# Rotary embedding by pairs of rows: twelve pairs moved to TensorE, three PSUM banks, and transfers of two tiles

## The chip, the cores and the metric

The kernel runs on one core of one Trainium2 chip. The metric is the device time of one execution in microseconds; the figure for the kernel before is the median of three runs, 164.04 us. The profile is of one execution and counts from its first to its last instruction (its span).

The engines are named as in the profile: PE is TensorE (PEld its loading of weights), DVE is VectorE, ACT is ScalarE, POOL is GpSimd, SP is SyncE, which issues the large transfers. The transfers of all queues run on the core's 16 DMA engines. SBUF is the on-chip memory, of 128 partitions; PSUM is the small memory that TensorE writes, of eight banks, each of 512 fp32 values a partition.

## The reference

The input `x` is 16 x 512 x 1024 fp32 (33.6 MB); every row of 1024 is 16 heads of 64. `cos` and `sin` are 512 x 32, one row for each position.

```python
x = x.reshape(batch, seq, num_heads, head_dim)
x1, x2 = x[..., :half_dim], x[..., half_dim:]
cos = cos[None, :, None, :]
sin = sin[None, :, None, :]
rotated = np.concatenate([x1 * cos - x2 * sin, x1 * sin + x2 * cos], axis=-1)
```

With the two halves of each head swapped, this is one product and one sum for each element: `out = x * cos + swapped(x) * (-sin, +sin)`. Every byte is read once and written once.

## The kernel before

**Tiles.** A tile is two batches (`BP = 2`): 64 partitions for each, and 8 rows (`R = 8`) of 1024 in each partition, so 8192 fp32 or 32 KB a partition and 4.19 MB a tile. There are eight tiles (`NT`) and five SBUF buffers for them (`NB`, `bufs` at L80). The result is written over `x` in the buffer and stored from there. Tiles 5, 6 and 7 are loaded into the buffers of tiles 0, 1 and 2 once these are stored.

**Groups of rows.** Within a tile the 8 rows are cut into two groups of three rows (`G = 3`, 3072 elements a partition) and one of two, called "pair" (2048); in the last tile the pair comes first (`ROWS`, `LAST`).

**The operations.** `swapped(x) * table` is called T for a group of three and B for the pair (`second`, L151). POOL makes it from `sns`, a table of (-sin, +sin) in SBUF; in tile 0 DVE makes B from `snp`, two rows of the same table in PSUM. Then there are two ways to finish a group:

- P and S on DVE (`vector`, L162): P puts `x * cos` into a PSUM tile `pp` (L171), S adds T or B and writes `x` (L174).
- A and then TensorE, for the pair of the tiles in `ONPE` (1, 3, 4, 5, 6): A multiplies `x` by the cosines in place (L168). `pe_rows` (L182) then takes chunks of 512 columns, adds `x` and B by two matmuls with the identity matrix into one PSUM bank `ps` (L188, L189), and ScalarE copies the bank to `x` (L190). `prow` holds one bank, so a chunk's first matmul waits for the copy of the chunk before.

That is five times four chunks on TensorE. The cosines stay in PSUM (`cos_ps`): every DVE operation has one operand in PSUM.

**Start.** The tables are loaded on ACT's queue (L97, L98), spread over the 128 partitions by two small products on TensorE (L117), and ScalarE makes the signed sines (L125, L126).

**Order.** The schedule is manual: each engine runs its instructions in the order of the program. `GPO` and `DVO` give POOL's and DVE's order for each tile. Semaphore waits follow from the data. `CARRY` (L174 and on) adds waits so that one wait covers several; the small `memset` of `both` (L206) makes DVE's first P wait for POOL, the spread and ScalarE; `AHEAD` (L230) makes POOL's T2 of four tiles wait for the next tile's load.

**Transfers.** SP issues them in the order of the program: loads of tiles 0 to 4 (tile 0 in three pieces, of 0.26, 1.31 and 2.62 MB, tile 1 in two), the stores of tiles 0, 1 and 2 when each is done, the loads of tiles 5, 6 and 7, the stores of 3 to 7 (the last in two pieces). A load into a used buffer waits until the store has landed, and everything behind it on SP waits too. That is 20 transfers on SP and 2 on ACT.

Of the kernel before, what the change touches and what calls it, by code (L numbers as in the profile page):

```python
# [7 lines left out]
FP32 = mybir.dt.float32  # L8
ALU = mybir.AluOpType
# [3 lines left out]
def kernel(  # L13
# [8 lines left out]
    nc = tc.nc  # L22
    P = nc.NUM_PARTITIONS
    batch, seq, dim = x.shape
    nh = num_heads
    hd = dim // nh
    half = hd // 2


    BP = 2  # L30
    HP = P // BP
    R = seq // HP
    NT = batch // BP
    assert HP * R == seq and BP * NT == batch
    NB = 5
    G = 3

    ROWS = {"1": (0, G), "2": (G, G), "pair": (2 * G, R - 2 * G)}

    LAST = {"pair": (0, R - 2 * G), "1": (R - 2 * G, G), "2": (R - G, G)}  # L40

    ONPE = (1, 3, 4, 5, 6)

    GPO = [("T1", "T2")] + [("B", "T1", "T2") if t in (2, 4, 7) else ("T1", "B", "T2") for t in range(1, NT)]

    DVO = [("P1", "S1", "P2", "B", "S2", "P3", "S3"), ("A", "P1", "S1", "P2", "S2"),
           ("P1", "S1", "P2", "S2", "P3", "S3"), ("A", "P1", "S1", "P2", "S2"), ("P1", "S1", "P2", "A", "S2"),
           ("P1", "S1", "P2", "A", "S2"), ("P1", "A", "S1", "P2", "S2"), ("P3", "S3", "P1", "S1", "P2", "S2")]

    CARRY = {(0, "P1"): "both", (0, "P2"): "T2", (1, "A"): "B", (3, "A"): "B", (4, "A"): "T2", (5, "P1"): "T1", (5, "A"): "T2",  # L50
             (6, "A"): "B", (7, "P3"): "B"}

    AHEAD = (1, 2, 3, 5)
# [7 lines left out]

    fixed = ctx.enter_context(tc.tile_pool(name="fixed", bufs=1))
    xin = ctx.enter_context(tc.tile_pool(name="xin", bufs=1))
    tpool = ctx.enter_context(tc.tile_pool(name="tpool", bufs=2))
    bpool = ctx.enter_context(tc.tile_pool(name="bpool", bufs=2))
    ptab = ctx.enter_context(tc.tile_pool(name="ptab", bufs=1, space=bass.MemoryType.PSUM))
    pgrp = ctx.enter_context(tc.tile_pool(name="pgrp", bufs=1, space=bass.MemoryType.PSUM))
    prow = ctx.enter_context(tc.tile_pool(name="prow", bufs=1, space=bass.MemoryType.PSUM))

    ctx.enter_context(tc.manual_schedule())  # L70

    SYNC = mybir.DependencyInfo(mybir.DependencyClass.Sync, mybir.DependencyReason.DATA)
# [7 lines left out]
    bufs = [xin.tile([P, R * dim], FP32, name=f"x{i}_sb") for i in range(NB)]  # L80
    x_tiles = [bufs[t % NB] for t in range(NT)]
    loads = [None] * NT
    stores = [None] * NT
    copies = [[] for _ in range(NT)]
    H = dim // 2

    def load(t, cuts=(0, 2 * R)):
        loads[t] = [nc.sync.dma_start(out=x_tiles[t][:, a * H:b * H], in_=xv[t][:, a * H:b * H])  # L88
                    for a, b in zip(cuts, cuts[1:])]

    def store(t, *parts):
        stores[t] = [nc.sync.dma_start(out=ov[t][:, a * H:b * H], in_=x_tiles[t][:, a * H:b * H])
                     for a, b in parts or ((0, 2 * R),)]

    load(0, (0, 1, 2 * G, 2 * R))
    tabs = fixed.tile([HP, 2, R * half], FP32, name="tabs")
    nc.scalar.dma_start(out=tabs[:, 1], in_=sinv)  # L97
    nc.scalar.dma_start(out=tabs[:, 0], in_=cosv)  # L98
    load(1, (0, 2 * G, 2 * R))
    for t in range(2, NB):  # L100
        load(t)


    ident = fixed.tile([P, P], FP32, name="ident")
    nc.gpsimd.memset(ident, 0.0)  # L105
    nc.gpsimd.affine_select(  # L106
        out=ident, in_=ident, compare_op=ALU.not_equal, fill=1.0,
# [4 lines left out]
    nc.gpsimd.tensor_copy(out=sel.rearrange("k (b p) -> k b p", b=BP),  # L112
                          in_=bass.AP(tensor=i64.tensor, offset=i64.offset, ap=[i64.ap[0], [0, BP], [1, HP]]))

    cos_ps = ptab.tile([P, R, half], FP32, name="cos_ps")
    sin_ps = pgrp.tile([P, G * dim], FP32, name="pp")[:, :R * half].rearrange("p (r j) -> p r j", r=R)
    spread = [nc.tensor.matmul(out=o.rearrange("p r j -> p (r j)"), lhsT=sel, rhs=tabs[:, i],  # L117
                               start=True, stop=True) for i, o in ((1, sin_ps), (0, cos_ps))]

    PR, PN = ROWS["pair"]  # L120
    sns = fixed.tile([P, R, 2, half], FP32, name="sns")
    snp = prow.tile([P, dim // 2], FP32, name="ps")
    signed = []
    for o, r0 in ((sns, 0), (snp[:, :PN * hd].rearrange("p (r s j) -> p r s j", r=PN, s=2), PR)):
        signed.append(nc.scalar.copy(out=o[:, :, 1, :], in_=sin_ps[:, r0:r0 + o.shape[1], :]))  # L125
        signed.append(nc.scalar.mul(out=o[:, :, 0, :], in_=sin_ps[:, r0:r0 + o.shape[1], :], mul=-1.0))  # L126

    def view(ap, r0, n):

        return ap[:, r0 * dim:(r0 + n) * dim]  # L130

    def cosb(r0, n):
        return bass.AP(tensor=cos_ps.tensor, offset=cos_ps.offset + r0 * half,
                       ap=[cos_ps.ap[0], [half, n], [0, 2 * nh], [1, half]])

    def snsb(tab, r0, n):

        return bass.AP(tensor=tab.tensor, offset=tab.offset + r0 * hd,
                       ap=[tab.ap[0], [hd, n], [0, nh], [1, hd]])

    def swapped(xt, r0, n):
        return bass.AP(tensor=xt.tensor, offset=xt.offset + r0 * dim + half,
                       ap=[xt.ap[0], [hd, n * nh], [-half, 2], [1, half]])

    Ts, TIs = {}, {}
    both = fixed.tile([1, 1], FP32, name="both")

    def span(t, o):
        return (LAST if t == NT - 1 else ROWS).get(o[-1]) or (LAST if t == NT - 1 else ROWS)["pair"]

    def second(eng, t, o):  # L151

        r0, n = span(t, o)
        pool = bpool if o == "B" else tpool
        Ts[t, o] = pool.tile([P, n * dim], FP32, name=o[0])
        tab = snsb(snp, r0 - PR, n) if eng is nc.vector else snsb(sns, r0, n)
        TIs[t, o] = eng.tensor_tensor(out=Ts[t, o], in0=swapped(x_tiles[t], r0, n), in1=tab, op=ALU.mult)  # L157
        return TIs[t, o]

    pps = {}  # L160

    def vector(t, o):  # L162
        r0, n = span(t, o)
        xr = view(x_tiles[t], r0, n)
        if o == "B":
            i = second(nc.vector, t, o)
        elif o == "A":
            i = nc.vector.tensor_tensor(out=xr, in0=xr, in1=cosb(r0, n), op=ALU.mult)  # L168
        elif o[0] == "P":
            pps[o[1]] = pgrp.tile([P, G * dim], FP32, name="pp")[:, :n * dim]  # L170
            i = nc.vector.tensor_tensor(out=pps[o[1]], in0=xr, in1=cosb(r0, n), op=ALU.mult)  # L171
        else:
            T = Ts[t, "B" if o == "S3" else "T" + o[1]]
            i = nc.vector.tensor_tensor(out=xr, in0=T, in1=pps[o[1]], op=ALU.add)  # L174
        if (t, o) in CARRY:
            after(i, TIs[t, CARRY[t, o]])
        implied(i, *loads[t], *spread, *signed)
        if t >= NB:
            implied(i, *loads[t - NB], *stores[t - NB], *copies[t - NB])
        return i  # L180

    def pe_rows(t):  # L182

        xr = view(x_tiles[t], PR, PN)
        for c in range(2 * PN):
            ps = prow.tile([P, dim // 2], FP32, name="ps")
            xc = xr[:, c * H:(c + 1) * H]
            nc.tensor.matmul(out=ps, lhsT=ident, rhs=xc, start=True, stop=False)  # L188
            nc.tensor.matmul(out=ps, lhsT=ident, rhs=Ts[t, "B"][:, c * H:(c + 1) * H], start=False, stop=True)  # L189
            i = nc.scalar.copy(out=xc, in_=ps)  # L190
            implied(i, *loads[t], *([As[t]] if t in As else []))
            if t >= NB:
                implied(i, *loads[t - NB], *stores[t - NB], *copies[t - NB])
            copies[t].append(i)

    def after(inst, other):
        tc.add_manual_dep(inst.ins, other.ins.name, SYNC, reason="brings the wait to the engines behind")

    As = {}

    def compute(t):
        for o in GPO[t]:
            i = second(nc.gpsimd, t, o)
            if (t, o) == (0, "T1"):

                TIs[0, "both"] = nc.gpsimd.memset(both, 0.0)  # L206
                after(TIs[0, "both"], signed[-1])
                after(TIs[0, "both"], spread[1])
        for o in DVO[t]:
            i = vector(t, o)  # L210
            if o == "A":
                As[t] = i
        if t in ONPE:
            pe_rows(t)

    for t in range(NB):
        compute(t)
        if t < NT - NB:
            store(t)
    for t in range(NB, NT):  # L220
        load(t)
    for t in range(NT - NB, NB):
        store(t)
    for t in range(NB, NT):
        compute(t)
        if t == NT - 1:
            store(t, (0, 2 * (R - G)), (2 * (R - G), 2 * R))
        else:
            store(t)
    for t in AHEAD:  # L230
        for l in loads[t + 1]:
            after(TIs[t, "T2"], l)


# [33 lines left out]
```

## Time and profile before

| | us |
|---|---|
| runs | 162.93, 164.04, 164.66 |
| median | 164.04 |
| span of the profiled execution | 162.0 |
| DVE busy | 134.1 (83%) |
| POOL busy | 138.9 (86%) |
| PE busy | 54.6 (34%) |
| ACT busy | 14.0 (9%) |
| the queue of the large transfers, share of 16 engines | 97.2% |
| the last S of DVE ends / span ends | 153.1 / 162.0 |

The page gives the span of the profiled execution and no other time of it. It moved 33.69 MB in and 33.55 MB out, 415 GB/s over the span. A group's line reads: line of the program, engine, operation, output <- inputs, shapes, how many | total busy time, mean of one in ns | idle time of the engine just ahead of them and what ended it. "PEclk" is the granted clock of TensorE in tenths of full speed. In SP's view, most of the waiting ahead of stores is for DVE's last S of the tile (93.9 us in nine waits), some for ScalarE's copies (29.1 us in three).

### The profile page before, as it was taken

What the parts mean: (1) busy time and instruction counts of PE and PEld (TensorE: products, weight loads), DVE (VectorE), ACT (ScalarE), POOL (GpSimd) and SP (SyncE); (2) the same over time, 40 slices, a digit from 0 to 9 for tenths busy, and PEclk for the clock granted to TensorE, in tenths of its full rate; (3) what the DMA queues carried; (4) which work ended last, traced back from release to release, by engine and by line L of the source; (5) the groups of instructions that cost most, each with busy time, mean ns of one, the idle gap of its engine ahead of it and who ended that gap; (6) DMA issues with size and microseconds to landing.
All of it is one profiled execution on the core that took longest, in us unless ns stands there. A gap on an engine that the chain in (4) does not pass through costs nothing.

```text
span 162.0 us, 381 instructions
## 1 busy us (share of the span) xinstructions
PE 54.6 (34%) x84; PEld 18.0 (11%) x84; DVE 134.1 (83%) x44; ACT 14.0 (9%) x25; POOL 138.9 (86%) x31
## 2 busy tenths in 40 slices
PE   0230000008680000038640009863988686400000
PEld 0110000002220000022110002220222132100000
DVE  0004999999999999999999999998968999999800
ACT  3200000000211000001210000021011212100000
POOL 2199999979999999999999999999999999992000
PEclk9999999999998555556995555599555899975555
DMA  6999999999999999998999999998999999799995
GB/s 190 392 456 403 425 496 388 461 445 388 461 445 388 404 502 388 421 485 388 429 453 396 445 461 396 461 437 372 453 445 404 396 396 453 332 388 518 384 409 243
DMA packets 3040, 67.24 MB, mean 415 GB/s; under 512 B 352, under 2 KB 480, under 8 KB 608
## 3 DMA queue, kind: packets, MB, share of 16 engines
q1 hardware_dynamic: 2880, 67.11, 97.2%
q10 hardware_dynamic: 160, 0.13, 0.2%
HBM read 33.69 MB, written 33.55 MB: 415 GB/s over the span
## 4 chain that ended last, share of the span: by engine, by line
DVE 33%; issue 26%; PE 19%; POOL 8%; ACT 4%; DMA 4%; SPq 0%; DVEq 0%; POOLq 0%
DVE x_sb L174 15%; DVE pp L171 13%; PE ps L188 11%; PE ps L189 9%; POOL T L157 6%; ACT x_sb L190 4%; DMA x_sb<-in_x_dram 4%; POOL B L157 3%; DVE x_sb L168 3%; DVE B L157 1%; SPq L88 0%; POOL both L206 0%; POOLq L157 0%; DVEq L174 0%; DVEq L171 0%
## 5 line engine op out<-in xcount | busy, mean ns | idle before, releaser
L157 POOL TENSOR_TENSOR T<-x_sb,sns 128x3072 f32<-128x3072 f32 x16 | 107.0, 6717 | 7.2 <-DMA x_sb<-in_x_dram 6.9
L171 DVE TENSOR_TENSOR pp<-x_sb,cos_ps 128x3072 f32<-128x3072 f32 (+1 forms) x19 | 60.7, 3193 | 15.2 <-POOL both L206 14.4
L188 PE MATMUL ps<-x_sb,ident 128*128 128x512 f32 x40 | 29.0, 815 | 76.6 <-issue 39.6
L174 DVE TENSOR_TENSOR x_sb<-T,pp 128x3072 f32<-128x3072 f32 x16 | 53.6, 3352 | 1.0
L157 POOL TENSOR_TENSOR B<-x_sb,sns 128x2048 f32<-128x2048 f32 x7 | 31.9, 4561 | 0.0
L189 PE MATMUL ps<-B,ident 128*128 128x512 f32 x40 | 26.7, 756 | 0.0
L190 ACT COPY x_sb<-ps 128x512 f32<-128x512 f32 x20 | 11.7, 585 | 121.9 <-PE ps L189 121.9
L188 PEld LDWEIGHTS ps<-x_sb,ident 128*128 128x128 f32 x40 | 7.4, 231 | 98.1 <-issue 68.8
L168 DVE TENSOR_TENSOR x_sb<-x_sb,cos_ps 128x2048 f32<-128x2048 f32 x5 | 11.4, 2285 | 2.8 <-POOL B L157 2.2
L189 PEld LDWEIGHTS ps<-B,ident 128*128 128x128 f32 x40 | 9.7, 241 | 13.4 <-issue 13.4
L174 DVE TENSOR_TENSOR x_sb<-B,pp 128x2048 f32<-128x2048 f32 x3 | 6.9, 2286 | 0.1
L117 PE MATMUL pp<-tabs,sel 64*128 64x256 f32 x2 | 1.2, 694 | 4.3 <-DMA tabs<-in_sin_dram 4.3
L117 PE MATMUL cos_ps<-tabs,sel 64*128 64x256 f32 x2 | 1.2, 713 | 4.1 <-DMA tabs<-in_cos_dram 4.1
L157 DVE TENSOR_TENSOR B<-x_sb,ps 128x2048 f32<-128x2048 f32 x1 | 2.3, 2281 | 0.0
L125 ACT ACT_TABLE_LOAD x1 | 1.3, 1283 | 1.9 <-issue 1.9
L117 PEld LDWEIGHTS cos_ps<-tabs,sel 64*128 64x128 f32 x2 | 0.5, 308 | 4.8 <-DMA tabs<-in_cos_dram 4.8
L117 PEld LDWEIGHTS pp<-tabs,sel 64*128 64x128 f32 x2 | 0.5, 310 | 4.3 <-issue 4.3
L125 ACT COPY sns<-pp 128x256 f32<-128x256 f32 x1 | 0.4, 372 | 2.3 <-PE pp L117 2.3
L105 POOL MEMSET ident<- 128x128 f32 x1 | 0.2, 204 | 0.3 <-POOLq L249 0.3
L126 ACT ACTIVATE sns<-pp 128x256 f32<-128x256 f32 x1 | 0.4, 390 | 0.0
L106 POOL TENSOR_SCALAR_AFFINE_SELECT ident<-ident 128x128 f32<-128x128 f32 x1 | 0.3, 292 | 0.1
L112 POOL COPY sel<-ident 64x128 f32<-64x128 f32 x1 | 0.3, 282 | 0.1
(7 smaller groups left out, 1.0 us busy)
## 6 DMA issues: line engine op xcount, KB each, us to landing
out_dram<-x_sb SPq DMA_DIRECT2D x7, 4096.0 KB, 20.5
x_sb<-in_x_dram SPq DMA_DIRECT2D x6, 4096.0 KB, 30.2
x_sb<-in_x_dram SPq DMA_DIRECT2D x2, 2560.0 KB, 16.4
out_dram<-x_sb SPq DMA_DIRECT2D x1, 2560.0 KB, 11.1
x_sb<-in_x_dram SPq DMA_DIRECT2D x1, 1536.0 KB, 15.2
out_dram<-x_sb SPq DMA_DIRECT2D x1, 1536.0 KB, 7.9
x_sb<-in_x_dram SPq DMA_DIRECT2D x1, 1280.0 KB, 6.3
x_sb<-in_x_dram SPq DMA_DIRECT2D x1, 256.0 KB, 3.0
```

The lines of the kernel that those rows point to most:

```text
L106: nc.gpsimd.affine_select(out=ident, in_=ident, compare_op=ALU.not_equal, fill=1.0, base=0, pattern=[[-1, P]], channel_multiplier=1,)
L112: nc.gpsimd.tensor_copy(out=sel.rearrange("k (b p) -> k b p", b=BP), in_=bass.AP(tensor=i64.tensor, offset=i64.offset, ap=[i64.ap[0], [0, ...
L117: spread = [nc.tensor.matmul(out=o.rearrange("p r j -> p (r j)"), lhsT=sel, rhs=tabs[:, i], start=True, stop=True) for i, o in ((1, sin_ps ...
L125: signed.append(nc.scalar.copy(out=o[:, :, 1, :], in_=sin_ps[:, r0:r0 + o.shape[1], :]))
L126: signed.append(nc.scalar.mul(out=o[:, :, 0, :], in_=sin_ps[:, r0:r0 + o.shape[1], :], mul=-1.0))
L157: TIs[t, o] = eng.tensor_tensor(out=Ts[t, o], in0=swapped(x_tiles[t], r0, n), in1=tab, op=ALU.mult)
L168: i = nc.vector.tensor_tensor(out=xr, in0=xr, in1=cosb(r0, n), op=ALU.mult)
L171: i = nc.vector.tensor_tensor(out=pps[o[1]], in0=xr, in1=cosb(r0, n), op=ALU.mult)
L174: i = nc.vector.tensor_tensor(out=xr, in0=T, in1=pps[o[1]], op=ALU.add)
L188: nc.tensor.matmul(out=ps, lhsT=ident, rhs=xc, start=True, stop=False)
L189: nc.tensor.matmul(out=ps, lhsT=ident, rhs=Ts[t, "B"][:, c * H:(c + 1) * H], start=False, stop=True)
L190: i = nc.scalar.copy(out=xc, in_=ps)
```

## The change

All work goes by pairs of rows: `G = 2`, so a tile is four pairs, 0 to 3, of 2048 elements a partition. A string for each tile (`PLAN`) gives the order of its operations on all engines; a letter is the operation (T on POOL, B the same on DVE, P and S and A as before, M the matmuls and copies of one pair) and the digit the pair. `GPO`, `DVO`, `ROWS`, `LAST`, `CARRY`, `AHEAD` and `both` go.

- M runs two pairs of tiles 1 to 6 and, as the plan is written, one of tile 7. M is four chunks; each adds T first and `x` second. `prow` holds three banks instead of one; `pp` needs four, and the cosines and `snp` share one bank (`tab`).
- T and B share one pool of five buffers of 2048 elements (before: two of 3072 and two of 2048).
- The five tile buffers are one SBUF tile (`slots`), so that neighbours can be moved together: the load of tiles 3 and 4, and the stores of 0 and 1, 3 and 4, 5 and 6 are single transfers of 8.39 MB (`load2`, `store2`). Tile 0 is loaded in two halves, the second behind the tables; tile 7 is stored in two pieces (pairs 0 to 2, pair 3). That is 14 transfers on SP and 2 on ACT.

```diff
-    G = 3
+    G = 2
+    C = 512
...
+    PLAN = ["T0 P0 T1 S0 P1 S1 B3 T2 P3 S3 P2 S2",
+            "T0 T1 A0 M0 B3 T2 A1 M1 P3 S3 P2 S2",
+            "T0 T1 T2 T3 A0 M0 A1 M1 P2 S2 P3 S3",
+            "T0 T1 A0 M0 B3 T2 A1 M1 P3 S3 P2 S2",
+            "T0 T1 T2 T3 A0 M0 A1 M1 P2 S2 P3 S3",
+            "T0 T1 A0 M0 B3 T2 A1 M1 P3 S3 P2 S2",
+            "T0 T1 T2 T3 A0 M0 A1 M1 P2 S2 P3 S3",
+            "T0 T1 T2 A0 M0 B3 P1 S1 P2 S2 P3 S3"]
...
-    tpool = ctx.enter_context(tc.tile_pool(name="tpool", bufs=2))
-    bpool = ctx.enter_context(tc.tile_pool(name="bpool", bufs=2))
+    tpool = ctx.enter_context(tc.tile_pool(name="tpool", bufs=5))
...
-    prow = ctx.enter_context(tc.tile_pool(name="prow", bufs=1, space=bass.MemoryType.PSUM))
+    prow = ctx.enter_context(tc.tile_pool(name="prow", bufs=3, space=bass.MemoryType.PSUM))
...
+    def load2(t):
+        loads[t] = loads[t + 1] = [nc.sync.dma_start(out=slots[:, t % NB:t % NB + 2], in_=pair(xv, t))]
+    def store2(t):
+        stores[t] = stores[t + 1] = [nc.sync.dma_start(out=pair(ov, t), in_=slots[:, t % NB:t % NB + 2])]
...
-    load(0, (0, 1, 2 * G, 2 * R))
+    load(0, (0, 4))
...
-    load(1, (0, 2 * G, 2 * R))
-    for t in range(2, NB):
-        load(t)
+    load(0, (4, 8))
+    load(1)
+    load(2)
+    load2(3)
...
+        for c in range(G * dim // C):
+            ps = prow.tile([P, C], FP32, name="ps")
+            xc = xr[:, c * C:(c + 1) * C]
+            made.append(nc.tensor.matmul(out=ps, lhsT=ident, rhs=Ts[t, k][:, c * C:(c + 1) * C],
+                                         start=True, stop=False))
+            made.append(nc.tensor.matmul(out=ps, lhsT=ident, rhs=xc, start=False, stop=True))
+            made.append(nc.scalar.copy(out=xc, in_=ps))
...
     for t in range(NB):
         compute(t)
-        if t < NT - NB:
-            store(t)
+        if t == 1:
+            store2(0)
+        elif t == 2:
+            store(2)
     for t in range(NB, NT):
         load(t)
-    for t in range(NT - NB, NB):
-        store(t)
+    store2(3)
     for t in range(NB, NT):
         compute(t)
-        if t == NT - 1:
-            store(t, (0, 2 * (R - G)), (2 * (R - G), 2 * R))
-        else:
-            store(t)
+        if t == 6:
+            store2(5)
+    store(7, (0, 6), (6, 8))
```

More of the change, by code (lines that the diff above doesn't have):

```diff
@@ L33 @@
     NT = batch // BP
-    assert HP * R == seq and BP * NT == batch
     NB = 5
-    G = 3
[L38 to L53, printed above, removed]
+    G = 2
+    C = 512
+    assert HP * R == seq and BP * NT == batch and R == 4 * G
+    PLAN = ["T0 P0 T1 S0 P1 S1 B3 T2 P3 S3 P2 S2",
[7 rows of a table added]
     xv = x.rearrange("b (p r) d -> (b p) (r d)", r=R)
@@ L77, in implied, with load, pair, store @@
             tc.declare_no_dep(inst.ins, o.ins, reason="implied by an earlier wait of the engine")
[L80 to L93, printed above, removed]
-    load(0, (0, 1, 2 * G, 2 * R))
+    F = R * dim
+    slots = xin.tile([P, NB, F], FP32, name="x_sb")
+    x_tiles = [slots[:, t % NB] for t in range(NT)]
+    loads = [[] for _ in range(NT)]
+    stores = [[] for _ in range(NT)]
+    def load(t, *cuts):
+        for a, b in cuts or ((0, R),):
+            loads[t].append(nc.sync.dma_start(out=x_tiles[t][:, a * dim:b * dim], in_=xv[t][:, a * dim:b * dim]))
+    def pair(v, t):
+        return v[t:t + 2].rearrange("t p f -> p t f")
+    def load2(t):
+        loads[t] = loads[t + 1] = [nc.sync.dma_start(out=slots[:, t % NB:t % NB + 2], in_=pair(xv, t))]
+    def store2(t):
+        stores[t] = stores[t + 1] = [nc.sync.dma_start(out=pair(ov, t), in_=slots[:, t % NB:t % NB + 2])]
+    def store(t, *cuts):
+        for a, b in cuts or ((0, R),):
+            stores[t].append(nc.sync.dma_start(out=ov[t][:, a * dim:b * dim], in_=x_tiles[t][:, a * dim:b * dim]))
+    load(0, (0, 4))
     tabs = fixed.tile([HP, 2, R * half], FP32, name="tabs")
@@ L113 @@
                           in_=bass.AP(tensor=i64.tensor, offset=i64.offset, ap=[i64.ap[0], [0, BP], [1, HP]]))
-    cos_ps = ptab.tile([P, R, half], FP32, name="cos_ps")
+    tab = ptab.tile([P, C], FP32, name="tab")
+    cos_ps = tab[:, :R * half].rearrange("p (r j) -> p r j", r=R)
+    snp = tab[:, R * half:R * half + G * hd].rearrange("p (r s j) -> p r s j", r=G, s=2)
+    BP0 = 3
     sin_ps = pgrp.tile([P, G * dim], FP32, name="pp")[:, :R * half].rearrange("p (r j) -> p r j", r=R)
@@ L118 @@
                                start=True, stop=True) for i, o in ((1, sin_ps), (0, cos_ps))]
-    PR, PN = ROWS["pair"]
     sns = fixed.tile([P, R, 2, half], FP32, name="sns")
-    snp = prow.tile([P, dim // 2], FP32, name="ps")
     signed = []
-    for o, r0 in ((sns, 0), (snp[:, :PN * hd].rearrange("p (r s j) -> p r s j", r=PN, s=2), PR)):
+    for o, r0 in ((sns, 0), (snp, BP0 * G)):
         signed.append(nc.scalar.copy(out=o[:, :, 1, :], in_=sin_ps[:, r0:r0 + o.shape[1], :]))
         signed.append(nc.scalar.mul(out=o[:, :, 0, :], in_=sin_ps[:, r0:r0 + o.shape[1], :], mul=-1.0))
-    def view(ap, r0, n):
-        return ap[:, r0 * dim:(r0 + n) * dim]
@@ L132, in cosb @@
[L132 to L171, printed above, removed]
-        else:
[L173 to L194, printed above, removed]
@@ L196, in after, with rows @@
-    def after(inst, other):
-        tc.add_manual_dep(inst.ins, other.ins.name, SYNC, reason="brings the wait to the engines behind")
-    As = {}
-    def compute(t):
[L202 to L214, printed above, removed]
+    def rows(t, k):
+        return x_tiles[t][:, k * G * dim:(k + 1) * G * dim]
@@ new lines, in cosb, with snb, swapped, emit @@
+    def cosb(k):
+        return bass.AP(tensor=cos_ps.tensor, offset=cos_ps.offset + k * G * half,
+                       ap=[cos_ps.ap[0], [half, G], [0, 2 * nh], [1, half]])
+    def snb(tab, k):
+        return bass.AP(tensor=tab.tensor, offset=tab.offset + k * G * hd, ap=[tab.ap[0], [hd, G], [0, nh], [1, hd]])
+    def swapped(xr):
+        return bass.AP(tensor=xr.tensor, offset=xr.offset + half, ap=[xr.ap[0], [hd, G * nh], [-half, 2], [1, half]])
+    Ts, pps = {}, {}
+    def emit(t, op):
+        o, k = op[0], int(op[1])
+        xr = rows(t, k)
+        if o in "TB":
+            Ts[t, k] = tpool.tile([P, G * dim], FP32, name="T")
+            eng, tb = (nc.gpsimd, snb(sns, k)) if o == "T" else (nc.vector, snb(snp, k - BP0))
+            return [eng.tensor_tensor(out=Ts[t, k], in0=swapped(xr), in1=tb, op=ALU.mult)]
+        if o == "P":
+            pps[t, k] = pgrp.tile([P, G * dim], FP32, name="pp")
+            return [nc.vector.tensor_tensor(out=pps[t, k], in0=xr, in1=cosb(k), op=ALU.mult)]
+        if o == "S":
+            return [nc.vector.tensor_tensor(out=xr, in0=Ts[t, k], in1=pps[t, k], op=ALU.add)]
+        if o == "A":
+            return [nc.vector.tensor_tensor(out=xr, in0=xr, in1=cosb(k), op=ALU.mult)]
+        made = []
+        for c in range(G * dim // C):
[5 more added lines that the diff above has]
+            made.append(nc.scalar.copy(out=xc, in_=ps))
+        return made
@@ L216 @@
+    done = [[] for _ in range(NT)]
+    def compute(t):
+        for op in PLAN[t].split():
+            for i in emit(t, op):
+                if t and op[0] != "T":
+                    implied(i, *loads[t])
+                if t >= NB:
+                    implied(i, *loads[t - NB], *stores[t - NB], *done[t - NB])
+                done[t].append(i)
     for t in range(NB):
         compute(t)
-        if t < NT - NB:
-            store(t)
+        if t == 1:
+            store2(0)
+        elif t == 2:
+            store(2)
@@ L220 @@
     for t in range(NB, NT):
         load(t)
-    for t in range(NT - NB, NB):
-        store(t)
+    store2(3)
     for t in range(NB, NT):
         compute(t)
-        if t == NT - 1:
-            store(t, (0, 2 * (R - G)), (2 * (R - G), 2 * R))
-        else:
-            store(t)
-    for t in AHEAD:
-        for l in loads[t + 1]:
-            after(TIs[t, "T2"], l)
+        if t == 6:
+            store2(5)
+    store(7, (0, 6), (6, 8))
 _INS = ['x', 'cos', 'sin', 'num_heads']
```

## The prediction

> **What bounds the kernel now.** I read the page's slices and queues first, then the busy time and rate by stretches, then the groups by shape, then TensorE's timeline. In the page, the two rows of the 40 slices and the queue line carry the answer:
>
> ```profile
> span 162.0 us, 381 instructions
> ...
> PE 54.6 (34%) x84; PEld 18.0 (11%) x84; DVE 134.1 (83%) x44; ACT 14.0 (9%) x25; POOL 138.9 (86%) x31
> ...
> PEclk9999999999998555556995555599555899975555
> DMA  6999999999999999998999999998999999799995
> ...
> q1 hardware_dynamic: 2880, 67.11, 97.2%
> ```
>
> The chain that ended last names DVE (33%), but it follows one line of releases. The DMA row is at 9 from end to end: the 16 engines are full, and no compute engine is. The stretches (columns: engines' busy time, granted clock, DMA share, GB/s) show how full:
>
> ```profile
> 2.20:51.20 49.00, 12.12 (x20) 4.21 (x20) 36.39 (x13) 4.35 (x9) 42.39 (x9) 1.00 1.02 429
> 51.20:139.00 87.80, 41.91 (x64) 13.82 (x64) 83.84 (x28) 8.78 (x15) 87.76 (x15) 0.67 1.00 428
> 139.00:140.00 1.00, 0.53 (x2) 0.00 (x0) 0.96 (x2) 0.43 (x1) 1.00 (x1) 1.00 0.30 131
> 140.00:141.00 1.00, 0.00 (x0) 0.00 (x0) 1.00 (x1) 0.15 (x1) 1.00 (x2) 1.00 0.08 33
> 141.00:153.00 12.00, 0.00 (x0) 0.00 (x0) 11.76 (x4) 0.00 (x0) 5.81 (x1) 0.61 1.01 431
> ```
>
> Loads alone and the later mix both move 428 GB/s. The one hole is at 139 to 141, where the queue is empty until tile 6's last ScalarE copy lets its store go: (1 - 131/428) + (1 - 33/428) = 1.6 us. Filled, it would leave a span of 160.4. So the question for the change is not how busy each engine is but when each store can be issued, against when the queue runs empty.
>
> TensorE's timeline shows what the moved work costs (start, length; x2 is two passes of one 512-column matmul):
>
> ```profile
> 37.02 2.05 PE L188 MATMUL ps<-x_sb,ident 128*128 128x512 f32 x2 [26.20 <-DVE x_sb L168]
> 38.86 1.92 PE L189 MATMUL ps<-B,ident 128*128 128x512 f32 x2
> 41.45 1.13 PE L188 MATMUL ps<-x_sb,ident 128*128 128x512 f32 x2 [0.67 <-ACT x_sb L190]
> 42.41 1.02 PE L189 MATMUL ps<-B,ident 128*128 128x512 f32 x2
> ...
> 47.73 0.59 PE L189 MATMUL ps<-B,ident 128*128 128x512 f32 x1
> ```
>
> Fast, a second pass follows 1.02 - 0.59 = 0.43 us after the first; slow, the starts 37.02 and 38.86 give 0.92, of which the first pass's lead is some 0.07, so 0.86. Four passes make a chunk, with a lead of about 0.1. With one bank, 0.67 us pass between chunks while ScalarE copies.
>
> The unit costs of a pair (2048 elements a partition) are in the groups by shape:
>
> ```profile
> L157 POOL TENSOR_TENSOR B<-x_sb,sns 128x2048 f32<-128x2048 f32 x7 | 31.9, 4561 | 0.0
> ...
> L168 DVE TENSOR_TENSOR x_sb<-x_sb,cos_ps 128x2048 f32<-128x2048 f32 x5 | 11.4, 2285 | 2.8 <-POOL B L157 2.2 <-POOL T L157 0.5
> ```
>
> By start to start in the timelines I use 4.49 us for POOL and 2.29 for DVE.
>
> **The change, part by part.** Each price below is a time against the 162.0 span. The page gives no other time of that execution; the span lies 2.0 below the median of the runs (164.04), and I carry those 2.0 over.
>
> *Work by engine.* The plan has 27 T on POOL (27 x 4.49 = 121 us, from 139), 56 operations on DVE (56 x 2.29 = 128, from 134) and 13 M, not twelve: 52 chunks against 20. That is 208 passes, 89 us fast or 179 slow, and 52 copies of 0.585 = 30 us on ScalarE. POOL and DVE keep some 30 us free, hidden under the transfers; TensorE is safe only while its clock is up. Tile 7's extra M (7 us) ends near 137, before DVE's last S at 147, so it costs nothing.
>
> *Three banks instead of one.* The 0.67 us wait per chunk goes, as a copy (0.585) fits in one chunk (1.8). A pair is then 16 x 0.43 + 4 x 0.1 = 7.3 us fast, 13.8 slow; with one bank it would be 4 x 2.66 = 10.6 (starts 41.45, 44.11).
>
> *Start.* The first load is 2.10 MB instead of the 1.57 that released POOL at 7.68: 0.52 MB at 412 to 428 GB/s is 1.2 us, T0 at 8.8. `both` (which held DVE to 14.39) is gone. P0 needs the cosine spread (done 10.8) and perhaps ScalarE's four sign operations behind it, as sine pair and cosine now share a bank: 11.5, bounds 10.8 and 12.5. DVE starts 2.9 us earlier; by itself this is worth nothing, as the queue is full then. AHEAD and CARRY waits go, and cost now 0.9 us on POOL at 33.3 and little else.
>
> *Queue.* 14 transfers on SP instead of 20. Each issue is 0.33 to 0.55 us in parallel with moving bytes: nothing. The rows stay 32 KB and each packet takes its usual time on its engine, so I keep 428 GB/s. A landing is seen 1.7 us after the last byte (load 2's bytes end near 31.6 by the rate, and POOL waits for it until 33.30). Tile 3 is released only with tile 4, when the loads end (51.2 + 1.7 = 52.9); POOL gets to it near 60: nothing.
>
> *First pair store (the new place 1).* The loads' bytes end at 51.2, as before. Before, store 0 stood in the queue from 34.75; after, nothing can follow until tiles 0 and 1 are both done (behind it on SP wait store 2 and loads 5 to 7, which could not go earlier anyway). DVE runs tile 0's nine operations and tile 1's A0 without a gap: 11.5 + 10 x 2.29 = 34.4. M0's first matmul has run by then (it needs only T0), so 30 passes are left of M0 and M1. TensorE is slow at first; in the trace the fast passes came between 4.4 and 13.3 us after a burst's start (41.45 after 37.02; 126.91 after 113.57), where the copies' gaps left TensorE idle a seventh of the time. Without gaps I take 5 us, near the shortest: 6 slow passes, then 24 x 0.43 + 0.7 = 11, M1 ends at 50.5, its copy at 51.1, first byte 0.8 later (140.2 to 141.0 now): 51.9. **Hole: 0.7 us.** Bounds: 0 with four slow passes or fewer; 4.7 if slow for 13 us.
>
> The Trainium skill, "TensorE: Matmul & The Clock Gate" (Part 1), says that a free-running window of some 3.4 us decides: one busy window raises the clock, an idle one lowers it. A burst without gaps would so be slow for 3.4 to 6.8 us, and the hole 0 to 1.5. The trace agrees for its first two bursts (4.4 us each) and not for the fourth (13.3), whose windows were not full.
>
> *Middle.* Store 0-1 moves from 51.9 to 71.5, store 2 (ready near 65) to 81.3, load 5 (issued when store 0-1 has landed, 73.2) to 91.1, load 6 to 100.9, load 7 to 110.7; store 3-4 is ready near 97 and moves until 130.5. No hole. Five buffers now couple POOL to TensorE: T1 and T2 of tile 2 wait for M0 and M1 of tile 1, some 4.5 us together, paid out of POOL's 30.
>
> *Second pair store (place 2).* Counted from tile 5's landing L: T0 ends at L + 4.5, DVE's seven operations at L + 20.5, tile 6's A0 at L + 22.8; M0 (14 passes left) at L + 29.2, M1 at L + 36.4, copy L + 37.1, first byte L + 37.9. The queue holds loads 6 and 7 and store 3-4 until (L - 1.7) + 39.2 = L + 37.5. **Hole: 0.4 us.** Bounds: 0, and 2.9 if the clock drops in TensorE's 2 us wait for A0 (5 us slow is 2.5 more).
>
> *Tail.* Stores 5-6 move until 150.6; tile 7 is ready at 142.9 (three pairs) and 147.4: no hole, where before the last S set the end.
>
> *Sum.* 162.0 - 1.6 (old hole) + 0.7 + 0.4 = 161.5; with the 2.0 around it, **163.5 us**, 0.3% under the median.
>
> **The rivals.** One per cent, 1.64 us, is about what a measurement of this kernel can tell from no change (its three runs spread over 1.73).
>
> *Pair stores held back by a slow clock (slower).* TensorE is the last to finish both tiles that a pair store waits for, with no slack. If the clock takes the 13 us of the fourth burst, hole 1 is 4.7 and the time 162.4 + 4.7 + 0.4 = 167.5; if it drops ahead of tile 6, hole 2 is 2.9 and the time 166.0; both, 170. It decides from 3.3 us of holes in all (162.4 + 3.3 = 165.7, 1% over the median). For: each of the four bursts of the trace began slow. Against: they began after 26, 22, 14 and 2.7 us of idling and ran with gaps; after the change the waits ahead of M0 are 2 us or less, but for tile 1's.
>
> *The queue never empties.* Both holes 0: span 160.4, time 162.4, 1% faster. It needs TensorE fast after four passes at place 1, and fast throughout at place 2. More is not to be had: 67.24 MB at 428 are 157.1 us.
>
> *TensorE as the bound.* If its clock stays down for most of the run, 208 passes are 179 us and the buffers stop POOL: over 215 us. Against: from 126.9 to 139.6 the passes are fast without a break at three quarters busy.
>
> *Pair transfers move slower.* They interleave two tiles 4 MB apart, row by row. The trace has none; against it stand 428 GB/s whatever the direction. The four hold 33.5 MB, 78 us: each 5% less is 4 us. The Trainium skill, "DMA: Bandwidth & Descriptors" (Latency and other measured facts), reports half rate for rows at a pitch of 4 MiB; here the rows that move together lie 32 KB apart as before, and no run shows such a case.
>
> **How the numbers follow.** Likeliest, 0.57: holes of up to 3.3 us in all, time 162.5 to 165.7; predicted 163.5. Slow clock at one or both stores 0.27 (166 to 170). Queue never empty 0.08. TensorE or waits that I do not see as the bound 0.06; slower pairs 0.02. So faster by over 1% 0.08, within 1% 0.57, slower 0.35. The range runs from the floor, 162.3, to 168.0, which takes in the greater part of the slow clock and leaves some 0.15 to 0.2 out.
>
> **What would show it.** Right: DMA near 430 GB/s except short holes near 51 and 130; store 0-1 released by ScalarE's copy of tile 1 at 50 to 52; passes 0.43 apart within a few us of each burst; POOL with idle time in tile 2 on TensorE; no hole in the last 20 us. Wrong: a clock row of 5 through the bursts, a hole over 2 us at either place, packets of the pair transfers longer than those of single ones, or a DMA row below 9 anywhere else.

## The result, and the profile after

The changed kernel takes 167.43 us (median of four runs, 166.55 to 168.68) against 163.49 for the kernel before (four runs); the ratio is 1.0261, with a 95% interval of 1.0213 to 1.0309. The forecast was 163.5, a little faster than the kernel before; the changed kernel is 2.6% slower, near the upper end of the range that was given (162.3 to 168.0). The profiled execution has a span of 166.5 us, 4.5 more than that of before. More than half of the 62 executions of the kernel before that were timed beside the experiments have a span of 160.7 us or less, so the profiled one, at 162.0, is a long one.

The page, with the rows that answer to those shown of before:

```profile
span 166.5 us, 687 instructions
...
PE 100.6 (60%) x212; PEld 42.2 (25%) x212; DVE 126.2 (76%) x56; ACT 32.8 (20%) x57; POOL 122.4 (74%) x34
...
PEclk9999999999999999999999996599999999955555
DMA  5999989999992998989998989999989989898981
...
q1 hardware_dynamic: 2528, 67.11, 95.3%
q10 hardware_dynamic: 160, 0.13, 0.2%
q8 instruction: 1, 0.02, 0.0%
q14 instruction: 1, 0.01, 0.0%
```

TensorE's 212 passes are four for the tables and 208 for thirteen pairs, one pair more than the title says. Its clock is up nearly throughout, and DVE and POOL are less busy than before: the engines did what the forecast said. The DMA row has a 2 at one place (near 52) and more 8s behind it, and the last slice holds a 1: transfers still run there, but hardly any. Two lines are new, q8 and q14 "instruction": one packet of 16 KB, which started at 75.9, and one of 8 KB, at 132.7. The stretches show the three places. The columns are those of the prediction; a packet counts where it starts, so single microseconds are lumpy:

```profile
51.00:52.00 1.00, 1.00 (x4) 0.47 (x3) 1.00 (x1) 0.59 (x1) 1.00 (x1) 1.00 0.16 66
52.00:53.00 1.00, 1.00 (x4) 0.48 (x3) 1.00 (x2) 0.04 (x1) 1.00 (x1) 1.00 0.00 0
53.00:54.00 1.00, 1.00 (x3) 0.38 (x2) 1.00 (x1) 0.55 (x1) 1.00 (x1) 1.00 0.00 0
...
82.00:83.00 1.00, 0.72 (x2) 0.48 (x3) 1.00 (x2) 0.00 (x0) 1.00 (x1) 1.00 1.92 524
83.00:84.00 1.00, 1.00 (x3) 0.38 (x3) 1.00 (x1) 0.56 (x1) 1.00 (x1) 1.00 0.08 33
...
161.00:163.00 2.00, 0.00 (x0) 0.00 (x0) 0.00 (x0) 0.00 (x0) 0.00 (x0) 0.50 0.95 397
163.00:165.00 2.00, 0.00 (x0) 0.00 (x0) 0.00 (x0) 0.00 (x0) 0.00 (x0) 0.50 0.07 29
```

In the kernel before, the second of these places reads:

```profile
82.00:83.00 1.00, 1.00 (x3) 0.19 (x1) 1.00 (x1) 0.00 (x0) 1.00 (x1) 1.00 1.06 459
83.00:84.00 1.00, 0.05 (x1) 0.00 (x0) 1.00 (x1) 0.59 (x1) 1.00 (x1) 1.00 1.21 524
```

First, the queue is empty: the last packets of the loads end at 52.2, and the store's first packet starts at 54.5. Second, at 82 to 84, where store 2 ends and load 5 begins, hardly a packet starts in a whole microsecond, though both were queued long before. Third, from 163 to 165 the share is 0.07: that is one of 16 engines (0.06) moving its last packets alone.

How much each costs is in the records of the transfers. Each of the 16 DMA engines reports the end of its part of every transfer (a packet of 4 bytes), so the middle engine (median) and the last one can be followed apart. A tile is eight packets of 32 KB for each engine, and takes 9.68 us (8 x 1.21) where nothing holds it up. What the median engine takes above 9.68 a tile, from the end of one transfer to the end of the next, is lost:

| | before | after | difference |
|---|---|---|---|
| around the empty queue (near 140; near 53), median engine | 1.8 | 2.7 | 0.9 |
| at the two turns, store to load (near 82) and load to store (near 112), median engine | 0.1 | 1.7 | 1.6 |
| last engine behind the median engine at the end | 0.1 | 2.0 | 1.9 |
| last byte of the last engine | 160.7 | 165.1 | 4.4 |

The three differences add up to the whole between these two executions. Only the first is a term of the forecast's sum.

Why the queue was empty for longer is at the start of the trace. TensorE's first products need the sine and then the cosine table, and DVE's first P needs both (first TensorE, then DVE):

```profile
8.86 1.19 PE L120 MATMUL pp<-tabs,sel 64*128 64x256 f32 x2 [8.86 <-DMA tabs<-in_sin_dram]
12.05 1.22 PE L120 MATMUL tab<-tabs,sel 64*128 64x256 f32 x2 [2.00 <-DMA tabs<-in_cos_dram]
...
36.88 2.08 PE L163 MATMUL ps<-x_sb,ident 128*128 128x512 f32 x2 [6.00 <-DVE x_sb L156]
38.75 1.91 PE L161 MATMUL ps<-T,ident 128*128 128x512 f32 x2
40.46 1.92 PE L163 MATMUL ps<-x_sb,ident 128*128 128x512 f32 x2
42.16 1.32 PE L161 MATMUL ps<-T,ident 128*128 128x512 f32 x2
43.32 1.02 PE L163 MATMUL ps<-x_sb,ident 128*128 128x512 f32 x2
44.18 1.02 PE L161 MATMUL ps<-T,ident 128*128 128x512 f32 x2
```

```profile
13.77 2.30 DVE L152 TENSOR_TENSOR pp<-x_sb,tab 128x2048 f32<-128x2048 f32 x1 [13.77 <-ACT tab L126]
```

In the kernel before, the same two products:

```profile
4.30 1.19 PE L117 MATMUL pp<-tabs,sel 64*128 64x256 f32 x2 [4.30 <-DMA tabs<-in_sin_dram]
9.60 1.22 PE L117 MATMUL cos_ps<-tabs,sel 64*128 64x256 f32 x2 [4.12 <-DMA tabs<-in_cos_dram]
```

So the sine was there at 8.86 instead of 4.30. DVE began at 13.77, not at the 11.5 of the forecast, and everything up to the first pair store came that much later than forecast: M0's second matmul at 36.88 instead of 34.4, the store at 53.58 instead of 51.1, as SP's timeline says:

```profile
53.58 0.39 SPq L89 DMA_DIRECT2D out_dram<-x_sb  x1
67.31 0.36 SPq L93 DMA_DIRECT2D out_dram<-x_sb  x1
74.61 11.88 SPq L80 DMA_DIRECT2D x_sb<-in_x_dram  x3
96.07 37.16 SPq L89 DMA_DIRECT2D out_dram<-x_sb  x2
```

The slow clock, on which the forecast's rival rested, did as expected: the passes are slow from 36.88 to 42.2, 5.3 us, where 5 was taken.

### The profile page after: what moved, and what is told of

Its sections match the earlier page's. It is cut to its first block, busy times and chain, and to the rows that moved or that the text cites. A ratio compares the mean times of both kernels' runs of the same rounds, so it can differ in the third digit from the quotient of the medians.

```text
span 166.5 us, 687 instructions
## 1 busy us (share of the span) xinstructions
PE 100.6 (60%) x212; PEld 42.2 (25%) x212; DVE 126.2 (76%) x56; ACT 32.8 (20%) x57; POOL 122.4 (74%) x34
## 4 chain that ended last, share of the span: by engine, by line
DMA 32%; DVE 23%; POOL 12%; PE 10%; issue 8%; POOLq 4%; ACT 1%; ACTq 0%; DVEq 0%; SPq 0%
DMA x_sb<-in_x_dram 13%; DMA out_dram<-x_sb 13%; POOL T L149 12%; DVE x_sb L154 10%; DVE pp L152 10%; DMA tabs<-in_cos_dram 6%; PE ps L163 5%; PE ps L161 4%; POOLq L223 4%; DVE T L149 3%; DVE x_sb L156 1%; PE tab L120 1%; ACT x_sb L164 0%; ACTq L97 0%; ACT tab L126 0%
## 5 line engine op out<-in xcount | busy, mean ns | idle before, releaser
L149 POOL TENSOR_TENSOR T<-x_sb,sns 128x2048 f32<-128x2048 f32 x27 | 121.5, 4534 | 18.1 <-ACT sns L126 9.2
L161 PE MATMUL ps<-T,ident 128*128 128x512 f32 x104 | 57.4, 635 | 20.9 <-POOL T L149 20.9
L163 PE MATMUL ps<-x_sb,ident 128*128 128x512 f32 x104 | 56.8, 629 | 8.5 <-DVE x_sb L156 8.5
L152 DVE TENSOR_TENSOR pp<-x_sb,tab 128x2048 f32<-128x2048 f32 x19 | 43.6, 2293 | 14.1 <-ACT tab L126 13.8
L164 ACT COPY x_sb<-ps 128x512 f32<-128x512 f32 x52 | 30.5, 586 | 97.3 <-PE ps L163 97.3
L154 DVE TENSOR_TENSOR x_sb<-T,pp 128x2048 f32<-128x2048 f32 x19 | 43.4, 2287 | 1.6
L156 DVE TENSOR_TENSOR x_sb<-x_sb,tab 128x2048 f32<-128x2048 f32 x13 | 29.4, 2281 | 8.8 <-POOL T L149 8.8
L161 PEld LDWEIGHTS ps<-T,ident 128*128 128x128 f32 x104 | 20.9, 204 | 48.7 <-issue 25.1
L163 PEld LDWEIGHTS ps<-x_sb,ident 128*128 128x128 f32 x104 | 20.4, 200 | 37.5 <-issue 23.7
L149 DVE TENSOR_TENSOR T<-x_sb,tab 128x2048 f32<-128x2048 f32 x5 | 11.4, 2279 | 0.0
```

The source lines that it names most:

```text
L149: return [eng.tensor_tensor(out=Ts[t, k], in0=swapped(xr), in1=tb, op=ALU.mult)]
L152: return [nc.vector.tensor_tensor(out=pps[t, k], in0=xr, in1=cosb(k), op=ALU.mult)]
L154: return [nc.vector.tensor_tensor(out=xr, in0=Ts[t, k], in1=pps[t, k], op=ALU.add)]
L156: return [nc.vector.tensor_tensor(out=xr, in0=xr, in1=cosb(k), op=ALU.mult)]
L161: made.append(nc.tensor.matmul(out=ps, lhsT=ident, rhs=Ts[t, k][:, c * C:(c + 1) * C], start=True, stop=False))
L163: made.append(nc.tensor.matmul(out=ps, lhsT=ident, rhs=xc, start=False, stop=True))
```

## The experiments

Three losses, then, with a theory for each: (1) late tables lengthen the hole; (2) the hole makes all 16 engines restart in step, and in step they are slow at the turns; (3) TensorE's longer program is fetched during the run by one DMA engine, which stays behind. Rivals: transfers of two tiles are slow in themselves (for 1 and 2), the turns alone (for 3). In the table of records at the end of this section, all runs stand side by side.

**Tables early.** Only tile 0's first load is cut again, so that the tables queue behind rows of 2 KB at first:

```diff
-    load(0, (0, 4))
+    load(0, (0, 0.5), (0.5, 4))
```

> The changed kernel with tile 0's first load cut as before (0.26 MB first), so that the tables no longer queue behind rows of 16 KB. Theory, from the two traces: the changed kernel's 4.4 us later last byte is 0.9 of a longer hole at 52 (2.7 against 1.8 us), 1.6 of packets that all 16 engines move slowly at the two places where the queue turns from stores to loads and back (82 and 112), and 1.9 of one engine that falls behind the others. The hole is there because the tables landed 4.5 us later and DVE began at 13.8 instead of 11.5. So here DVE begins at 11.5 or before, store 0-1 is issued near 51.3, the hole is under 0.8 us and the time falls by 2 us (ratio to the kernel before near 1.013). If the slow packets come from the engines' restarting in step after the hole, they go too: 3.5 us less, ratio near 1.004. Rival: the pair transfers and the second pair store make the time, not the start: less than 1 us changes.

165.44 us, ratio 1.0117 (1.0034 to 1.0200; four runs, 164.41 to 166.2). TensorE's and DVE's first rows in this run:

```profile
3.98 1.19 PE L121 MATMUL pp<-tabs,sel 64*128 64x256 f32 x2 [3.98 <-DMA tabs<-in_sin_dram]
8.89 1.22 PE L121 MATMUL tab<-tabs,sel 64*128 64x256 f32 x2 [3.72 <-DMA tabs<-in_cos_dram]
```

```profile
10.62 2.29 DVE L153 TENSOR_TENSOR pp<-x_sb,tab 128x2048 f32<-128x2048 f32 x1 [10.62 <-ACT tab L127]
```

The sine lands 4.9 us earlier, DVE begins 3.2 us earlier, store 0-1 is issued at 49.34 and the queue does not run empty. The time falls by 2.0 us. In the profiled execution, the fastest of the four, the slow packets are gone too; the other three, up to 1.8 us slower, have no trace. The store of two tiles is still there, so by itself it makes neither the hole nor the slow packets: it takes the late tables as well. Loss 1 is shown.

**Stores 0 and 1 apart; all transfers single.** The first has `store(t)` for t below 3 in place of `store2(0)`, the second has also tiles 3, 4, 5 and 6 stored and 3 and 4 loaded by themselves:

```diff
-        if t == 1:
-            store2(0)
-        elif t == 2:
-            store(2)
+        if t < 3:
+            store(t)
...
-    load2(3)
+    load(3)
+    load(4)
```

> The changed kernel with tiles 0 and 1 stored by two transfers, each when its tile is done; all else as changed, tables late. Theory: store 0 is in the queue at 35, so there is no hole at 52: 2.5 to 2.7 us less; with the slow packets also gone, 4 us less (ratio near 1.0). Load 5 can be issued 10 us earlier, which is hidden. Rival (the late start of DVE is what counts, whatever the transfers): less than 1 us changes.

> The changed kernel with every tile loaded and stored by a transfer of its own, tables late. Theory: as the run with only tiles 0 and 1 apart, within 0.5 us, since no other pair transfer leaves a hole. Rival: moving two tiles row by row is slow in itself, so that the three other pair transfers cost too: more than 1 us below the run with only tiles 0 and 1 apart, and packets near 1.21 us in place of longer ones.

164.32 us (1.0049; 1.0018 to 1.0081) and 164.65 us (1.0071; 1.0038 to 1.0104). With late tables and no hole, 3 us are gone: it is not DVE's late start that costs, but what the first store can be issued against. The other three pair transfers change nothing beyond the intervals, although in the first of the two runs the store of tiles 3 and 4 was followed by 1.0 us of idling of the median engine: the engine that was behind used it to catch up (2.3 us behind before it, 1.3 after). Both runs are still slower than the kernel before, while their median engine ends before its median engine (159.6 and 158.6 against 160.6 in the profiled executions): one engine is 1.2 and 2.2 us behind.

**TensorE's code alone.** The kernel before, with 68 small matmuls more in TensorE's idle time:

```diff
+    def more(n):
+        ps = prow.tile([P, dim // 2], FP32, name="ps")
+        for _ in range(n):
+            nc.tensor.matmul(out=ps[:, :8], lhsT=ident, rhs=ident[:, :8], start=True, stop=True)
...
+        if t in (1, 3):
+            more(34)
```

> The kernel before with 68 matmuls of 8 columns (272 more instructions on TensorE, about as many as in the changed kernel) in its idle time after tiles 1 and 3; nothing reads what they write. Theory: TensorE's longer program is fetched during the run: a packet of 16 KB from a queue of its own shows near the middle, and the one DMA engine that moves it lands its part of each later transfer about 1 us after the others until the queue runs empty near 139, so the time rises by under 0.5 us. Rival: the lagging engine comes from the turns between stores and loads alone: no such packet here, and lags as in the kernel before.

164.70 us, ratio 1.0073 (1.0035 to 1.0111). The queue lines of its page now have a q8, where the page of the kernel before has q1 and q10 alone:

```profile
q1 hardware_dynamic: 2880, 67.11, 96.8%
q10 hardware_dynamic: 160, 0.13, 0.2%
q8 instruction: 1, 0.02, 0.0%
```

The packet came at 76.5 and took 1.01 us, in which only 15 engines moved rows; the row behind it took 1.61 us instead of 1.21. One engine was 0.3 us behind the median before it and 1.6 after, 2.3 from 110 on. The cost was larger than expected. In the profiled execution the queue never ran empty near 139, as TensorE was done with tile 6 by 135: the median engine ended at 158.7, the last at 160.9. In the profiled execution of before, the hole near 139 had let an engine that was 2.0 us behind catch up (1.1 at 140, 0.1 at 151). So a hole late in the queue hides such a lag, and a full queue shows it. But that execution came to its 2.0 us without a fetched packet: the lag grew by 0.5 us at the first turn, 0.2 at the next transfer and 1.1 at the second turn. The fetch is one way to such a lag, not the only one.

**The changed kernel once more**, and a control that failed.

> The changed kernel once more, to see which of its three losses recur in another execution. Theory: hole of 2 to 3 us near 52 (DVE begins near 13.8), a fetched packet of 16 KB near 75 and one DMA engine 2 us behind the others at the end; if restarting in step causes the slow packets, they are there again at 82 and 112 (0.8 us each on all engines). Rival: the slow packets were chance, and most executions lack them; then the last byte lands near 163.5.

167.20 us, ratio 1.0239 (1.0175 to 1.0303). All three losses are there again: hole, slow packets at both turns, an engine 1.9 us behind.

> All transfers of one tile, but the stores of tiles 0 and 1 both issued when tile 1 is done: the hole without a pair transfer. Theory: as the changed kernel (ratio near 1.02 to 1.026), with a hole of 2.7 us and, if the restart in step is their cause, slow packets at both turns. Rival: the pair transfers cause the slow packets; then only the hole costs (ratio near 1.02, no packets over 1.4 us on all engines at once).

This run had no hole, and so says nothing of one: store 0 waits only for tile 0's work, wherever it stands in the program, and went at 33.97. Its 164.42 us (1.0066; 1.0039 to 1.0094) repeat the run with single transfers. With a real wait on tile 1's last copy:

```diff
+            store(0)
+            tc.add_manual_dep(stores[0][0].ins, copied[1].ins.name, SYNC, reason="held until tile 1 is done")
+            store(1)
```

> All transfers of one tile, with the store of tile 0 made to wait for tile 1's last copy on ScalarE (in the run labelled k_hole the store of tile 0 still went at 34, so that one had no hole). Theory: the queue is empty for 1.5 to 3 us near 52, all engines restart within 0.1 us of each other, and the slow packets at both turns come back (0.7 to 0.9 us each): ratio 1.02 to 1.026, as the changed kernel. Rival: the pair transfers cause the slow packets; then only the hole is paid, the excess of packets at 80 to 90 and 110 to 120 stays under 0.2 us, and the ratio is 1.012 to 1.018.

168.12 us, ratio 1.0272 (1.0211 to 1.0332). No transfer moves two tiles, and yet all of the change's loss is there. The stretches of this run, around the hole and the second turn:

```profile
51.00:52.00 1.00, 1.00 (x4) 0.46 (x3) 1.00 (x2) 0.25 (x1) 1.00 (x1) 1.00 0.01 0
52.00:53.00 1.00, 1.00 (x3) 0.38 (x2) 1.00 (x1) 0.59 (x1) 1.00 (x1) 1.00 0.00 0
...
110.00:114.00 4.00, 4.00 (x11) 1.76 (x10) 3.86 (x3) 1.19 (x3) 4.00 (x2) 1.00 1.03 360
```

At 110 to 114 it moves 360 GB/s, much as the changed kernel does (352 in the same stretch). Loss 2 follows from the hole, not from the size of transfers: the run that differs from this one in the wait alone has no slow packets.

**Only the transfers.** The kernel before with its own computation and the pair transfers of the change.

```diff
-    for t in range(2, NB):
-        load(t)
+    load(2)
+    load2(3)
...
+        if t == 1:
+            store2(0)
+        elif t == 2:
+            store(2)
...
-    for t in range(NT - NB, NB):
-        store(t)
+    store2(3)
...
+        elif t == 6:
+            store2(5)
```

> The kernel before, its computation unchanged (five pairs on TensorE, one bank), with only the transfers of two tiles (load 3-4; stores 0-1, 3-4, 5-6). Theory: store 0-1 is ready near 49.5, so no hole there; store 5-6 is ready at 140 as in the kernel before, but tile 5 no longer fills the queue from 130 to 139, so a hole of 9 to 11 us opens there and the time rises by 8 to 10 us (ratio 1.05 to 1.06). Rival: transfers of two tiles are free, or gain by their size: within 1% of the kernel before.

171.63 us, ratio 1.0521 (1.0446 to 1.0595). From 134 to 138 nothing moves, while TensorE, DVE and POOL still work at tile 6:

```profile
132.00:134.00 2.00, 1.52 (x4) 0.68 (x4) 1.90 (x2) 0.43 (x1) 2.00 (x1) 1.00 0.61 262
134.00:136.00 2.00, 1.32 (x4) 0.49 (x3) 2.00 (x1) 0.59 (x1) 2.00 (x2) 1.00 0.00 0
136.00:138.00 2.00, 1.13 (x3) 0.19 (x1) 1.90 (x2) 0.58 (x1) 2.00 (x1) 1.00 0.00 0
138.00:140.00 2.00, 0.00 (x0) 0.00 (x0) 1.97 (x2) 0.00 (x0) 2.00 (x1) 1.00 1.08 459
```

The hole at 134 was expected to be 9 to 11 us and is 5.0: the queue ran empty at 133.6 instead of 130, and store 5-6 went at 137.8 instead of 140, as TensorE finished tile 6 earlier. Another of 1.8 us, not expected, opened at 52, since store 0-1 went only at 53.04, and slow packets (0.9 us) followed at the first turn; a third, of 0.7 us, lay at the second turn. So the pair transfers cost 8.5 us with the old computation, and with the change's computation about half of that.

**Fewer pairs on TensorE.** First early tables and single transfers with 13 pairs, then with 7, then with 5 (84 passes, as before; POOL makes 30 products and tile 7 is stored in three pieces).

> All transfers of one tile, and the first load cut as before, so that the tables land early. The hole is already gone without that cut, so theory says: as the run with single transfers (ratio 1.007), within 0.5 us; what is left over the kernel before is the one DMA engine that is 2 us behind. Rival: the late start of the engines costs also later; then 1 us or more below it.

> As the run before it in this list, with 7 pairs on TensorE instead of 13 (one in each of tiles 1 to 7, the others P and S on DVE: 62 operations there, 142 us). TensorE's program is 232 passes and weight loads instead of 424. Theory: no packet of 16 KB is fetched during the run, no engine lags by over 1 us for that reason, the last byte lands 1.2 us earlier and the ratio is 1.000 or a little below. DVE must end near 154, before the queue does. Rival: the lag has another cause and stays: ratio 1.007; or DVE becomes the bound: last store issued after 156.

> Pairs of rows, three banks, single transfers, early tables, but five pairs on TensorE (tiles 1 to 5): 84 passes, as many as in the kernel before. POOL makes 30 products (143 us), DVE 61 operations; tile 7 is stored in three pieces. In all runs so far a packet of 16 KB came when TensorE had done 86 to 93 passes. Theory: no such packet here, no engine over 1 us behind from it, no hole above 1 us: span 160.3 to 161, ratio 0.995 to 1.0. Rival: the packet comes by time or by all engines' instructions: it is here too, ratio 1.005.

164.22 us (1.0059; 1.0030 to 1.0088), 163.56 us (1.0002; 0.9975 to 1.0029) and 163.01 us (0.9974; 0.9946 to 1.0003). With 13 pairs and no hole, the early tables bring nothing clear, as expected (164.22 against 164.65 with late ones). With 7 pairs the packet came after all, at 114, when TensorE had done 86 passes; one engine fell 1.4 us behind, and a hole near 149, where tile 7 was late, let it catch up. So that run's expectation of no packet was wrong, and its time does not show a kernel without one. With 5 pairs there is no packet of 16 KB. One engine is 0.6 to 0.7 us behind from 8.5 us on and catches up in 0.8 us of idling before the last store; at the end none is behind. Its page:

```profile
span 161.0 us, 412 instructions
...
PE 54.0 (34%) x84; PEld 20.1 (13%) x84; DVE 138.7 (86%) x61; ACT 14.1 (9%) x25; POOL 135.6 (84%) x37
...
DMA  5999999999999999999999999999999999999976
```

This kernel is at best 0.5% faster than the kernel before and perhaps the same; its runs lie closer together (162.81 to 163.18 in ten, against 162.90 to 164.66).

The records of the profiled executions, in us. "Hole" is the time near 52 in which at most two engines moved anything (other holes are in the text); "turns" is the time above 1.216 us a packet of 32 KB, summed over 80 to 90 and 110 to 120 and divided by 16; "fetch" is when the 16 KB packet started; the last columns are the ends of the median and the last engine.

| run | hole | turns | fetch | median | last |
|---|---|---|---|---|---|
| before | 0 | 0.0 + 0.0 | none | 160.6 | 160.7 |
| after | 2.3 | 0.8 + 0.8 | 75.9 | 163.1 | 165.1 |
| after, again | 1.4 | 0.7 + 0.9 | 74.9 | 162.3 | 164.1 |
| single, store 0 held | 1.8 | 0.9 + 0.8 | 75.2 | 162.4 | 164.7 |
| old computation, pair transfers | 1.8 | 0.9 + 0.0 | none | 168.0 | 168.1 |
| tables early | 0 | 0.0 + 0.0 | 72.1 | 159.2 | 160.9 |
| stores 0, 1 apart | 0 | 0.0 + 0.0 | 75.0 | 159.6 | 160.8 |
| all single | 0 | 0.0 + 0.0 | 75.0 | 158.6 | 160.8 |
| all single, once more (store 0 not held) | 0 | 0.0 + 0.0 | 73.7 | 158.6 | 160.5 |
| before, more code | 0 | 0.0 + 0.0 | 76.5 | 158.7 | 160.9 |
| 13 pairs, early, single | 0 | 0.0 + 0.0 | 71.4 | 158.7 | 160.4 |
| 7 pairs | 0 | 0.0 + 0.0 | 114.0 | 160.3 | 160.4 |
| 5 pairs | 0 | 0.0 + 0.0 | none | 159.6 | 159.7 |

All four runs with a hole at 52 have the slow packets at the first turn, and none of the nine others has. The packet of 16 KB came when TensorE had done 86 to 93 passes, at times from 71 to 114; the kernel before ends at 84.

## Why the prediction was wrong

**Held.** What bounds the kernel (the queue, 428 GB/s, counted by when a store can be issued); the passes at 0.43 us and the slow start of 5 us (5.3); POOL's idle time in tile 2 on TensorE (3.1 us against 4.5); the second pair store, issued by 133.2 with the queue not empty (hole 0 against 0.4); the tail (last store issued near 150.7, under the running transfers). Of the rivals, the slow clock did not happen, TensorE was not the bound, and the pair transfers were not slower in themselves: with early tables and pair stores the packets took their usual time. The page that reports half rate at a pitch of 4 MiB (Trainium skill, "DMA: Bandwidth & Descriptors", Latency and other measured facts) thus describes another pattern than two tiles 4 MB apart moved row by row.

**Failed: the step "Start".** The step took the tables' landing as unchanged and put P0 at 11.5, with bounds of 10.8 and 12.5; it was 13.77. The same step had costed the larger first piece only by its bytes (1.2 us for POOL). The tables are on another queue but on the same 16 engines, and their small rows waited between rows of 16 KB instead of 2 KB. The Trainium skill, "DMA: Bandwidth & Descriptors" (Queues, rings and completion order), says that an engine goes round its queues a packet at a time, and the traces fit that: the sine's product at 8.86 behind 16 KB rows, at 4.30 and 3.98 behind 2 KB rows. With 2.3 us more, the forecast's own chain gives a hole of 0.7 + 2.3 = 3.0; 2.7 was measured. The hole's mechanism was right; the landing of the tables, which was put at no change without a reason, mis-sized it. Luck is in the agreement: the end of the loads' bytes, 51.2, was worked out from the rate, and by the engines' own records the median engine ended at 52.1 before and 52.0 after. In the same way a landing is seen 0.6 us after the last engine's end (load 2: 32.69, and POOL goes on at 33.30), not 1.7.

**Failed: the step "Queue".** "Each packet takes its usual time" did not hold behind the hole: 1.7 us were lost at the two turns. That they follow from the hole is shown by the run with single transfers and store 0 held. Why is open. The restart in step fits the first turn: where it was slow, all engines had ended the transfer before within 0.09 us of the median; in the nine other runs the last was 0.14 us or more behind. It does not fit the second turn: there the changed kernel's last engine was 1.4 us behind and the others up to 0.19 us off the median, and the packets were slow all the same; with 7 pairs all lay within 0.21 us and the packets took their usual time. (The run with the old computation says nothing of the second turn, as its queue was empty there.) Why engines should be slow at a turn was not tried.

**Missing from the sum: the engine that is behind.** The sum has no term for one DMA engine that falls behind the others, and 208 passes were counted as TensorE's time, not as code that has to be moved. The fetch of that code put one engine 1.0 to 1.3 us behind in the seven runs without a hole at 52 that have it, and where the queue then stayed full to the end, the last engine ended late by that and more. That a longer program costs time by itself is shown by the kernel before with more code (0.35 to 1.11% slower). How much of the 1.9 us is the fetch is not shown. Near 112 the lag grew by another 0.4 to 1.1 us in these kernels (not with 7 pairs), in the kernel before by 1.1 without any fetch, with 5 pairs by next to nothing; this step's cause stays open. The profiled execution of before had hidden a lag of 2.0 in the very hole that the forecast took off as a gain.

**Failed: the term for the old hole, and the base.** The sum takes off 1.6 us for a hole that belonged to the one profiled execution: TensorE's burst at 113.57 stayed slow for 13.3 us in it, and tile 6's last copy ended at 140.1. In the run with the old computation and pair transfers the same burst was slow for only 4.0 us, and in the run with more code TensorE was done with tile 6 by 135. The usual span of the kernel before is 160.7, so the forecast's own span of 161.5 is 0.8 us above it, not below: the forecast of a small gain came from a long execution as the base. The 2.0 us that the prediction carried over are part of this: the 62 executions of the kernel before on record all take 2.41 to 2.55 us beyond their span, so the profiled one took some 164.5, more than the median of 164.04. That most executions lack the old hole is inferred from their spans; no trace of one is on record.

Between the two profiled executions, the measured sum is 162.0 - 1.8 (old hole) + 2.7 + 1.6 + 1.9 = 166.4, against a span of 166.5. Without the two unforeseen terms the forecast span would have been off mainly by its holes (1.1 us forecast, 2.7 measured).

## What to carry to other kernels

Where the DMA queue is full throughout, cost a change by the latest time at which each store may be issued, and add up what the queue loses, not what the engines gain. A small transfer that all engines wait for should not share the DMA engines with large rows when a store depends on it: cut the first large load so that its first rows are short. Here that gave 2.0 us with a store of two tiles, and nothing sure with single transfers. Count a long unrolled program among the transfers: in a full queue, a DMA engine that moves 16 KB of code ends its part of the next transfers late. And before a hole in one profile is booked as a gain, compare that execution's span with those of others.

## What the runs showed of the hardware

- The program of TensorE was fetched during the run, by one packet of 16 KB that took 0.92 to 1.03 us, when 86 to 93 passes were done. The Trainium skill, "Runtime: NRT & Kernel Launch" (Instruction fetch mechanics), says that code is refilled in blocks of 16 KiB and that the cost is mostly hidden. The size agrees; TensorE indeed did not wait (its matmuls follow at 0.86 us across the packet at 75.9 of the changed kernel), but the DMA engine's part of the loads and stores did, for 1.0 to 1.3 us.
- After an empty queue near 52, some 15 to 23 packets took 1.5 to 2.3 us instead of 1.21 where stores gave way to loads, some 30 us later (four runs of four; the cause is open).
- With three banks the gap between chunks vanished altogether once the clock was up: matmuls follow at 0.86 us (two passes), also from one chunk to the next, where the forecast had left 0.1 a chunk.
